# Two summing products turned round: one-pass transposes for the adaLN vectors, block-diagonal ones for the squares of queries and keys

## The chip, the core and the metric

The kernel runs on one NeuronCore of a Trainium2 chip. The metric is device time in microseconds (us), the median of the timed runs. The core's engines run side by side, each with its own instruction order fixed when the program is built: TensorE (PE in the profile, its weight loads PEld), VectorE (DVE), ScalarE (ACT), GpSimd (POOL) and SyncE (SP, which issues the transfers). They wait for each other through semaphores.

## The reference, cut to what matters

Two layers over 512 latent tokens with a prefix of 256 context tokens, width 1024: an attention layer, then a Mamba-2 layer, each followed by a gated feed-forward part. Before each part the activations are normalised and modulated by vectors that come from a conditioning vector:

```python
mod_l = jnp.split((silu_c @ ada_w[i] + ada_b[i])[:, None, :], 6, axis=-1)   # latent tokens
mod_c = jnp.split(silu_cc @ ada_w[i] + ada_b[i], 6, axis=-1)                # context tokens
h_l = modulate(rms_norm(x, norm_mix_w[i]), mod_l[0], mod_l[1])              # x * (1 + scale) + shift

# attention: each head of 64 of the queries (16 heads) and keys (4 heads) is normalised
q_l = rms_norm(q_l.reshape(bsz, seq, N_HEADS, HEAD_DIM), q_norm)
k_l = rms_norm(k_l.reshape(bsz, seq, N_KV_HEADS, HEAD_DIM), k_norm)
```

The change touches how the six modulation vectors of layer 0 are turned from a row into a column (five of them on TensorE), and how the squares of each head of 64 channels are summed for the norms of queries and keys.

## The kernel before, in words

Activations lie with channels on the 128 partitions and tokens along the free axis (512 latent, then 256 context). Large products run three times in a one-pass reduced type, on a high and a low part of each operand (`mm3`: lines L105, L106, L108); small ones run directly in float32, where the profile shows two weight loads and two products for each one in the program.

The first 72 us are the front of the attention layer, whose order on PE, ACT and DVE is written by hand (`manual_schedule`). A block of products `warm` runs while the first inputs arrive. Then, for each of the eight slabs m of 128 input channels: `ada` multiplies the conditioning vector (in `sc32`, columns 0 and 1 of 32: latent and context) with two blocks of 128 weight columns into the bank `ps_ada`, as four partial sums that lie on partitions 32j and 32j+1 for j = 0..3 (the k slabs of the contraction are dealt to four column strips of the array). DVE copies that to `ada_sb`. Then the four partial rows are added and turned into columns: one float32 product per 128 columns, with `ada_sb` as the stationary side and the 128x2 selector `g.sel` as the moving side, into `ps_adt` (L135). DVE adds the bias (`mod`, L146), forms the scale with the norm's weight (`moda`, L149) and modulates slab m of the activations: `ht` (L322, DVE), `hha` (L331, ACT), `hla` (L332, DVE). The six products `ps_l` of slab m consume `hha` and `hla`. The weights of each slab arrive as `wst` and are split into `wsh` (ACT) and `wsl` (POOL for seven slabs, DVE for the last). The same two steps run six more times in the attention stage for the other layer-0 vectors, as background jobs (`ps_ada` with 512 columns, four `ps_adt` products each).

From 72 us to about 330 us the order comes from a list scheduler with a cost model of its own: it places the context part `ps_c` of the projections, the values `ps_v`, the scores of each head pair (`ps_m` for their maxima, `ps_s`, exponentials `pr`), the product with the values (`ps_o`, L799: two products, one for each head of the pair, on the two halves of the array's columns), and in between the background jobs `ps_q`, `ps_ada`, `ps_adt` and the output projection `ps_d`. For each of ten pairs of heads (two of keys, eight of queries) `normed` squares the 128 channels on ACT and sums each head's 64 squares on TensorE into `ssq` (L677): a 64x64 block of ones for each head, 512 and then 256 columns, so four float32 products; the two heads' products lie on opposite quarters of the array. The later parts of the kernel are not touched.

Of the kernel before, what the change touches and what calls it, by code (L numbers as in the profile page):

```python
# [7 lines left out]
P = 128  # L8
F32 = mybir.dt.float32
# [3 lines left out]
AX = mybir.AxisListType  # L13
# [7 lines left out]
HD = 64  # L21
# [90 lines left out]
def ada(g, src, layer, chunks, m0, nm, big=True):  # L112


    nc = g.nc
    cols = nm * len(chunks) * P
    per = (1024 if big else T) // cols
    st = []
    for k0 in range(0, KT, per):
        n = min(per, KT - k0)  # L120
        t = t4(g, "wada") if big else t3(g, "wada")
        t = t[:, : n * cols].rearrange("p (k a b) -> p k a b", k=n, a=len(chunks))
        nc.sync.dma_start(t.rearrange("p k a b -> p (k a b)"), src[:, k0 * cols : (k0 + n) * cols])
        st += [t[:, k].rearrange("p a b -> p (a b)") for k in range(n)]
    yield 0
    ps = Bank(g, "ps_ada")
    for k in range(KT):
        j = k % 4
        nc.tensor.matmul(ps[32 * j : 32 * j + 32, 0:cols], g.sc32[:, k, :], st[k], start=k < 4, stop=k >= 4)
    sb = g.t3p.tile([P, 512], F32, tag="t2", bufs=6, name="ada_sb")  # L130
    nc.vector.tensor_copy(sb[:, 0:cols], ps[:, 0:cols])
    yield BREAK
    pt = Bank(g, "ps_adt")
    for i in range(cols // P):
        nc.tensor.matmul(pt[:, 2 * i : 2 * i + 2], sb[:, i * P : (i + 1) * P], g.sel, start=True, stop=True)  # L135
    for i, ch in enumerate(chunks):
        modulation(g, pt[:, 2 * nm * i : 2 * nm * (i + 1)].rearrange("p (m v) -> p m v", v=2), layer, ch, m0, nm)
    yield BREAK


def modulation(g, src, layer, ch, m0, nm, nv=2):

    nc = g.nc
    c0 = PC[f"adab{layer}"] + ch * KT + m0
    md = g.mod[layer][ch][:, m0 : m0 + nm, 0:nv]
    nc.vector.tensor_tensor(md, src, g.par[:, c0 : c0 + nm].unsqueeze(2).broadcast_to([P, nm, nv]), ALU.add)  # L146
    if ch in (1, 4):
        n0 = PC[("nmix" if ch == 1 else "nffn") + str(layer)] + m0
        nc.vector.scalar_tensor_tensor(g.moda[layer][ch][:, m0 : m0 + nm, 0:nv], md, 1.0,  # L149
                                       g.par[:, n0 : n0 + nm].unsqueeze(2).broadcast_to([P, nm, nv]),  # L150
                                       ALU.add, ALU.mult)
# [103 lines left out]
def ordered(g, bi, prev):  # L255

    if prev is not None:
        g.tc.add_manual_dep(bi.ins, prev.ins.name, mybir.DependencyInfo(
            mybir.DependencyClass.NoSync, mybir.DependencyReason.DATA), reason="place among products")
# [252 lines left out]
def attention(g, adas, project, X):  # L512


    nc, I = g.nc, g.I
# [45 lines left out]
    warm = Bk("warm")  # L561

    def busy(n):
        for _ in range(n):
            nc.tensor.matmul(warm[:, :P], g.ones, g.ones, start=True, stop=True)

    busy(38)
    acc = t3(g, "acc", n=L)
# [96 lines left out]
    def normed(qs, gain):  # L665

        sq = t3(g, "qsq")
        nc.scalar.activation(sq, qs, AF.Square)
        nc.scalar.activation(qs, qs, AF.Identity, scale=gain)
        sw = t2("qsw")  # L670
        for b in range(4):
            nc.sync.dma_start(sw[32 * (b ^ 1) : 32 * (b ^ 1) + 32], qs[32 * b : 32 * b + 32, :L])
        ss = []
        for c0, c1 in ((0, L), (L, T)):
            ps = Bk("ssq")
            for s in S64:
                ordered(g, nc.tensor.matmul(ps[s, : c1 - c0], g.ones[s, :HD], sq[s, c0:c1], start=True, stop=True), placed[0])  # L677
            ss.append((ps[:, : c1 - c0], slice(c0, c1)))
        nc.vector.tensor_tensor(qs[:, :L], qs[:, :L], g.cos, ALU.mult)
        nc.vector.tensor_tensor(sw, sw, g.sin, ALU.mult)  # L680
        nc.vector.tensor_tensor(qs[:, :L], qs[:, :L], sw, ALU.add)
        yield

        y, u = t3(g, "qy"), sq
        for ps, c in ss:
            nc.scalar.activation(y[:, c], ps, AF.Ln, scale=1.0 / HD, bias=eps64)
        nc.scalar.activation(y, y, AF.Exp, scale=-0.5)
        nc.scalar.activation(u, y, AF.Square)
        for ps, c in ss:
            nc.vector.scalar_tensor_tensor(u[:, c], ps, HD * EPS, u[:, c], ALU.add, ALU.mult)  # L690
        nc.vector.tensor_tensor(qs, qs, y, ALU.mult)
        nc.vector.scalar_tensor_tensor(qs, u, -3.0 * HD, qs, ALU.add, ALU.mult)
        yield
# [41 lines left out]
            nc.scalar.copy(qs[:, c0 : c0 + n], ps[:, :n])  # L735

    onesr = g.const.tile([P, P], F32R, name="onesr")
    nc.scalar.copy(onesr, g.ones)
    id2 = g.const.tile([P, HD], F32, name="id2")
    for h in S64:  # L740
        nc.gpsimd.tensor_copy(id2[h], g.ident[h, h])
# [796 lines left out]
def body(nc, tc, I, out, dbg=None):  # L1538
    g = Ctx()
# [16 lines left out]
    for m in range(0, KT, 2):  # L1556
# [1 line left out]
    nc.sync.dma_start(g.par, I["par"])  # L1558
    g.ident, g.blk, g.sel = (cst[:, a:b] for a, b in
                             ((CST_IDENT, CST_IDENT + P), (CST_BLK, CST_BLK + 2), (CST_SEL, CST_SEL + 2)))  # L1560
    g.ones = g.const.tile([P, P], F32, name="ones")
    nc.vector.memset(g.ones, 1.0)
    g.sc32 = g.const.tile([P, KT, 32], F32, name="sc32")
    nc.vector.memset(g.sc32, 0.0)
    tc.keep_in_program_order(nc.scalar.preload_act_table_set("natural_log_exp_and_others"))
# [154 lines left out]
```

## Time and profile before

| | |
|---|---|
| median of 3 runs | 1887.12 us (1885.73 to 1887.31) |
| span of the profiled execution, first to last instruction | 1884.5 us (its own time is not given apart from the span; the runs lie 1.2 to 2.8 us above it) |
| PE busy | 1860.0 us, 99% of the span, 10794 products |
| PEld / DVE / ACT / POOL busy | 81% / 72% / 44% / 12% |
| granted TensorE clock, mean | 1.000 |
| `ps_adt` on PE | 80 products, 16.4 to 283.0 us |
| `ssq` on PE | 80 products, 73.0 to 296.2 us |
| `warm` on PE | 98 products, 1.1 to 17.4 us |

A product's time in the table is from its start to its modelled end. Products overlap in the array, so what a product costs is the distance from its start to the next one's start, not its duration. In a timeline row the first number is the start in us, the second how long the merged group lasts, the numbers behind the operation its tile of the array (rows*columns) and the moving operand, and xN the number of merged instructions; the bracket gives the idle time of the engine before it and what ended that.

### The profile page before, as it was taken

The page shows a single profiled execution, that of the slowest core. Times are in us where ns is not written, and L with a number is a line of the kernel's source. Part 1 is how long each engine was busy: PE and PEld are TensorE (multiplying, and loading weights), DVE is VectorE, ACT ScalarE, POOL GpSimd, SP SyncE. Part 2 cuts the span into 40 slices and gives each one's busy share as a digit, 9 for nine tenths or more (in the row PEclk, how much of TensorE's full clock was granted, in tenths as well). Part 3 has the DMA queues.
Part 4 walks back from the last instruction along what each step waited for, and adds up shares of the span by engine and source line. Part 5 has one row for each costly group of instructions (what it writes and reads, how often), then busy time and mean ns, then how long its engine had stood idle before and what let it go on. Part 6 is the DMA issues. An engine that isn't in the chain of part 4 may idle for free.

```text
span 1884.5 us, 27447 instructions
## 1 busy us (share of the span) xinstructions
PE 1860.0 (99%) x10794; PEld 1531.3 (81%) x10794; DVE 1348.8 (72%) x2013; ACT 832.6 (44%) x1422; POOL 232.5 (12%) x220
## 2 busy tenths in 40 slices
PE   9999999999999999999999999999999999999999
PEld 7865545689888888888888888888887888888887
DVE  5688999678877777444478977777888676565655
ACT  3655544354222222222257577766667352323331
POOL 2100000030000000000031243443334200000000
PEclk9999999999999999999999999999999999999999
DMA  9223241015444554222224243434344323323332
GB/s 342 70 82 118 84 145 62 18 50 189 136 134 124 176 180 146 68 68 67 67 79 140 70 121 114 133 113 135 120 126 125 100 78 101 101 87 104 90 101 90
DMA packets 73489, 210.02 MB, mean 111 GB/s; under 512 B 8976, under 2 KB 14480, under 8 KB 73232
## 3 DMA queue, kind: packets, MB, share of 16 engines
q1 hardware_dynamic: 73360, 208.26, 35.2%
q8 instruction: 85, 1.39, 0.3%
q14 instruction: 44, 0.36, 0.1%
HBM read 198.79 MB, written 6.82 MB: 109 GB/s over the span
## 4 chain that ended last, share of the span: by engine, by line
PE 80%; DVE 10%; issue 4%; ACT 3%; DMA 2%; POOL 1%; SPq 0%; DVEq 0%; POOLq 0%; ACTq 0%
PE ps_up L105 10%; PE ps_up L106 10%; PE ps_up L108 10%; PE ps_d L105 6%; PE ps_d L108 6%; PE ps_d L106 5%; PE ps_in L105 4%; PE ps_in L108 4%; PE ps_in L106 3%; PE ps_o L799 2%; PE ps_s L835 2%; PE ps_st L1340 1%; DVE wl L87 1%; DVE xf L1212 1%; PE ps_wo L106 1%
## 5 line engine op out<-in xcount | busy, mean ns | idle before, releaser
L87 DVE TENSOR_TENSOR wl<-wst,wh 128x1024 fp32r<-128x1024 f32 x211 | 261.0, 1237 | 246.5 <-PE ps_up L106 125.4
L85 ACT CAST wh<-wst 128x1024 fp32r<-128x1024 f32 x211 | 220.8, 1048 | 413.5 <-DMA wst<-in_wup 316.2
L106 PE MATMUL ps_up<-hlf,wh 128*128 128x512 f32 x992 | 351.6, 354 | 0.0
L108 PE MATMUL ps_up<-hhf,wl 128*128 128x512 f32 x992 | 351.4, 354 | 0.0
L105 PE MATMUL ps_up<-hhf,wh 128*128 128x512 f32 x992 | 351.2, 355 | 0.0
L105 PEld LDWEIGHTS ps_up<-hhf,wh 128*128 128x128 f32 x992 | 187.5, 189 | 26.2
L106 PEld LDWEIGHTS ps_up<-hlf,wh 128*128 128x128 f32 x992 | 187.6, 189 | 26.0
L108 PEld LDWEIGHTS ps_up<-hhf,wl 128*128 128x128 f32 x992 | 187.5, 189 | 26.1
L105 PE MATMUL ps_in<-hhs,wh 128*128 128x512 f32 (+1 forms) x544 | 199.7, 367 | 0.0
L108 PE MATMUL ps_in<-hhs,wl 128*128 128x512 f32 (+1 forms) x544 | 193.5, 356 | 0.0
L106 PE MATMUL ps_in<-hls,wh 128*128 128x512 f32 (+1 forms) x544 | 193.3, 355 | 0.0
L108 PE MATMUL ps_d<-hdh,wl 128*128 128x512 f32 (+1 forms) x496 | 173.4, 350 | 0.0
L105 PE MATMUL ps_d<-hdh,wh 128*128 128x512 f32 (+1 forms) x496 | 173.3, 350 | 0.1
L106 PE MATMUL ps_d<-hdl,wh 128*128 128x512 f32 (+1 forms) x496 | 172.9, 349 | 0.0
L1022 DVE SCALAR_TENSOR_TENSOR X<-ps_d,mod,X 128x256 f32<-128x256 f32 (+1 forms) x176 | 102.7, 614 | 27.1 <-PE ps_d L108 27.0
L105 PEld LDWEIGHTS ps_in<-hhs,wh 128*128 128x128 f32 x544 | 102.8, 189 | 15.5 <-issue 1.9
L108 PEld LDWEIGHTS ps_in<-hhs,wl 128*128 128x128 f32 x544 | 102.7, 189 | 15.0
L106 PEld LDWEIGHTS ps_in<-hls,wh 128*128 128x128 f32 x544 | 102.9, 189 | 13.0
L106 PEld LDWEIGHTS ps_d<-hdl,wh 128*128 128x128 f32 x496 | 93.2, 188 | 14.4 <-DVE hdl L87 0.2
L108 PEld LDWEIGHTS ps_d<-hdh,wl 128*128 128x128 f32 x496 | 93.2, 188 | 13.1
L105 PEld LDWEIGHTS ps_d<-hdh,wh 128*128 128x128 f32 x496 | 93.0, 188 | 13.0 <-ACT hdh L85 0.3
L168 DVE SCALAR_TENSOR_TENSOR junk<-wada,cb 128x1024 f32<-128x1024 f32 x80 | 97.5, 1218 | 1.1 <-ACT cb L159 0.8
(375 smaller groups left out, 3632.9 us busy)
## 6 DMA issues: line engine op xcount, KB each, us to landing
wst<-in_wup SPq DMA_DIRECT2D x88, 512.0 KB, 3.5
wada<-in_adaT SPq DMA_DIRECT2D x56, 512.0 KB, 3.8
wst<-in_win SPq DMA_DIRECT2D x48, 512.0 KB, 3.6
wst<-in_wdown SPq DMA_DIRECT2D x44, 512.0 KB, 3.7
E<-ad SPq DMA_DIRECT2D x64, 256.0 KB, 6.7
wada<-in_adaB SPq DMA_DIRECT2D x24, 512.0 KB, 4.6
ec<-ead SPq DMA_DIRECT2D x64, 128.0 KB, 4.6
wst<-in_wout SPq DMA_DIRECT2D x16, 512.0 KB, 3.7
```

The source lines that it names most:

```text
L85: keep(nc.scalar.copy(hi, src))
L87: keep(eng.tensor_tensor(lo, src, _r(hi), ALU.subtract))
L105: mm(out, wh, ah, start=first, stop=False)
L106: mm(out, wh, al, start=False, stop=False)
L108: i = mm(out, wl, ah, start=False, stop=last)
L168: g.tc.keep_in_program_order(nc.vector.scalar_tensor_tensor(junk, w, 1.0, cb[:, v * D : (v + 1) * D], ALU.mult, ALU.mult, accum_out=md[:, ...
L799: nc.tensor.matmul(po[S64[e], :n], v, pr[:, 512 * e + off : 512 * e + off + n], start=first, stop=last)
L835: nc.tensor.matmul(outs[e], a[S64[e], k], b[S64[e], q], start=i == 0, stop=False)
L1022: nc.vector.scalar_tensor_tensor(ap, o[:, c0:c1], gate[:, m, v : v + 1], ap, ALU.mult, ALU.add)
L1212: i = nc.vector.scalar_tensor_tensor(cv, raw[:, tap : tap + n], par(f"sw{tap}", j), cv, ALU.mult, ALU.add)
L1340: nc.tensor.matmul(ps[:, d * 256 : (d + 1) * 256], Bt[:, t * P : (t + 1) * P], xw[d][t], start=t == ts[0], stop=t == ts[-1])
```

## The change

Modulation vectors: instead of the product with the selector, each 128 columns of `ada_sb` are transposed (`nc.tensor.transpose`, one instruction on PE where the product took two), and DVE adds the four partial sums of each vector straight out of PSUM with one `reduce_sum` per vector (22 in all) into `mod`. `modulation` then adds the bias with `mod` as input, in place, where its input was `ps_adt`.

Squares: a 128x128 matrix `heads` with two 64x64 blocks of ones on the diagonal replaces the two 64x64 products by one over the whole array. `heads` is made by three `memset`s on DVE. `ones` shrinks to 64 columns, `onesr` is therefore filled in two copies, and the products `warm` now use `heads` on both sides.

```diff
@@ ada
-        nc.tensor.matmul(pt[:, 2 * i : 2 * i + 2], sb[:, i * P : (i + 1) * P], g.sel, start=True, stop=True)
+        nc.tensor.transpose(pt[:, i * P : (i + 1) * P], sb[:, i * P : (i + 1) * P], g.ident)
+    quarters = pt[:, 0:cols].rearrange("p (m j r) -> p m r j", j=4, r=32)
     for i, ch in enumerate(chunks):
-        modulation(g, pt[:, 2 * nm * i : 2 * nm * (i + 1)].rearrange("p (m v) -> p m v", v=2), layer, ch, m0, nm)
+        md = g.mod[layer][ch][:, m0 : m0 + nm]
+        nc.vector.reduce_sum(md, quarters[:, nm * i : nm * (i + 1), 0:2], axis=AX.X)
+        modulation(g, md, layer, ch, m0, nm)
@@ attention, busy
-            nc.tensor.matmul(warm[:, :P], g.ones, g.ones, start=True, stop=True)
+            nc.tensor.matmul(warm[:, :P], g.heads, g.heads, start=True, stop=True)
@@ attention, normed
-            for s in S64:
-                ordered(g, nc.tensor.matmul(ps[s, : c1 - c0], g.ones[s, :HD], sq[s, c0:c1], start=True, stop=True), placed[0])
+            ordered(g, nc.tensor.matmul(ps[:, : c1 - c0], g.heads, sq[:, c0:c1], start=True, stop=True), placed[0])
@@ attention
-    nc.scalar.copy(onesr, g.ones)
+    for h in S64:
+        nc.scalar.copy(onesr[:, h], g.ones)
@@ body
-    g.ones = g.const.tile([P, P], F32, name="ones")
+    g.ones = g.const.tile([P, HD], F32, name="ones")
     nc.vector.memset(g.ones, 1.0)
+    g.heads = g.const.tile([P, P], F32, name="heads")
+    nc.vector.memset(g.heads, 0.0)
+    for h in (slice(0, HD), slice(HD, P)):
+        nc.vector.memset(g.heads[h, h], 1.0)
```

The scheduler also places some instructions elsewhere. Three places matter. The first is DVE in the hand-ordered front, slab 6, where `mod_86`/`mod_87` (after: `mod_90`/`mod_91`) are the shift and the scale. Before:

```order
L131 COPY ada_sb<-ps_ada 128x256
L146 TENSOR_TENSOR mod_86<-ps_adt,par 128x2
L146 TENSOR_TENSOR mod_87<-ps_adt,par 128x2
L149 SCALAR_TENSOR_TENSOR moda_98<-mod_87,par 128x2
L322 SCALAR_TENSOR_TENSOR ht<-X,moda_98,rsl 128x512
```

After:

```order
L131 COPY ada_sb<-ps_ada 128x256
L139 TENSOR_REDUCE mod_90<-ps_adt 128x2
L149 TENSOR_TENSOR mod_90<-mod_90,par 128x2
L139 TENSOR_REDUCE mod_91<-ps_adt 128x2
L149 TENSOR_TENSOR mod_91<-mod_91,par 128x2
L152 SCALAR_TENSOR_TENSOR moda_102<-mod_91,par 128x2
L325 SCALAR_TENSOR_TENSOR ht<-X,moda_102,rsl 128x512
```

Two instructions stand more between `ada_sb` and `ht`, and the two additions of the bias now read both inputs from SBUF (the row reads `mod,par` where it read `ps_adt,par`).

The second is PE in the attention stage near 256 to 262 us of the profile. `ps_o` is the product with the values, x2 the two heads of a pair. Before:

```order
L837 MATMUL ps_s<-diag_2389,onesr 128x512 x2
L799 MATMUL ps_o<-pr,v_752 64x512
L761 MATMUL ps_m<-kh_1991,qh 128x256 x4
L799 MATMUL ps_o<-pr,v_752 64x512
L835 MATMUL ps_s<-qh,kh_1991 128x512 x2
L835 MATMUL ps_s<-qh,kl_1992 128x512 x2
L835 MATMUL ps_s<-ql,kh_1991 128x512 x2
L837 MATMUL ps_s<-diag_2389,onesr 128x512 x2
L799 MATMUL ps_o<-pr,v_753 64x512
L761 MATMUL ps_m<-kh_1991,qh 128x512 x2
L799 MATMUL ps_o<-pr,v_753 64x512
```

After:

```order
L840 MATMUL ps_s<-diag_2397,onesr 128x512 x2
L764 MATMUL ps_m<-kh_2000,qh 128x256 x4
L802 MATMUL ps_o<-pr,v_772 64x512 x2
L838 MATMUL ps_s<-qh,kh_2000 128x512 x2
L838 MATMUL ps_s<-qh,kl_2001 128x512 x2
L838 MATMUL ps_s<-ql,kh_2000 128x512 x2
L840 MATMUL ps_s<-diag_2397,onesr 128x512 x2
L764 MATMUL ps_m<-kh_2000,qh 128x512 x2
L802 MATMUL ps_o<-pr,v_773 64x512 x2
```

Two pairs of `ps_o` that were parted by `ps_m` stand together now. The third is PE at the first background vector (near 163 us), where the opposite happens. Before:

```order
L837 MATMUL ps_s<-diag_1481,onesr 128x512 x2
L761 MATMUL ps_m<-kh_928,qh 128x512 x2
L135 MATMUL ps_adt<-cst,ada_sb 128x2 x4
L799 MATMUL ps_o<-pr,v_753 64x512 x2
L105 MATMUL ps_q<-hha_3_108,wh 128x512
```

After:

```order
L840 MATMUL ps_s<-diag_1492,onesr 128x512 x2
L802 MATMUL ps_o<-pr,v_773 64x512
L135 MATMUL ps_adt<-cst,ada_sb 128x128 x4
L764 MATMUL ps_m<-kh_945,qh 128x512 x2
L802 MATMUL ps_o<-pr,v_773 64x512
L105 MATMUL ps_q<-hha_3_112,wh 128x512
```

One pair of `ps_o` is parted by the four transposes and `ps_m`. At 62 to 64 us, where slab 7's `ps_l` products follow, 15 `ps_c` products stand ahead of the one that takes `hla` instead of 11. The order on SP and POOL is unchanged.

## The prediction

> **What bounds the kernel now.** I read the page first, then TensorE's waits by stage, then the timeline around the products that change.
>
> ```profile
> span 1884.5 us, 27447 instructions
> PE 1860.0 (99%) x10794; PEld 1531.3 (81%) x10794; DVE 1348.8 (72%) x2013; ACT 832.6 (44%) x1422; POOL 232.5 (12%) x220
> ```
>
> TensorE has work all the time, so a shorter product is worth its shortening wherever TensorE doesn't wait behind it. The waits in the two stages that change, 20 to 72 us and 72 to 330 us:
>
> ```profile
> PE ps_adt L135 <- DVE ada_sb L131: 1.3, 1, 1.3
> ...
> PE ps_l L106 <- DVE hla L332: 0.3, 1, 0.3
> ...
> PE ps_m L761 <- DVE ma L765: 3.3, 4, 1.2
> ```
>
> ```profile
> 110.00:330.00 220.00, 214.61 (x1336) 120.70 (x1334) 198.15 (x285) 115.19 (x154) 0.00 (x0) 1.00 0.31 102
> ```
>
> The first two rows are of the hand-ordered front and stand exactly on the chain that the change lengthens (modulation vector, then `ht`, `hha`, `hla`). The third is the largest wait of the attention stage, and the fourth row (columns: length, PE, PEld, DVE, ACT, POOL) says that TensorE is busy for 214.6 of 220 us there, DVE for 198.2. So the front is paced by DVE at two points, the attention stage by TensorE with a DVE close behind. Everything after 330 us only moves along.
>
> **Transposes in the attention stage** (six groups). Starts give the price:
>
> ```profile
> 187.19 1.08 PE L799 MATMUL ps_o<-pr,v 128*64 128x512 f32 x4
> 188.20 1.05 PE L135 MATMUL ps_adt<-cst,ada_sb 128*128 128x2 f32 x8
> 189.11 0.36 PE L105 MATMUL ps_q<-hha,wh 128*128 128x256 f32 x1
> 189.31 0.28 PE L106 MATMUL ps_q<-hla,wh 128*128 128x256 f32 x1
> 189.43 0.28 PE L108 MATMUL ps_q<-hha,wl 128*128 128x256 f32 x1
> ```
>
> ```profile
> 1017.32 1.47 PE L1314 MATMUL ps_xt<-cst,xf 128*128 128x128 f32 x12
> 1018.54 0.48 PE L105 MATMUL ps_in<-hhs,wh 128*128 128x512 f32 x1
> 1018.86 0.40 PE L106 MATMUL ps_in<-hls,wh 128*128 128x512 f32 x1
> 1019.09 0.40 PE L108 MATMUL ps_in<-hhs,wl 128*128 128x512 f32 x1
> ```
>
> From 188.20 to the second `ps_q` at 189.31 are 1.11 us; less 0.12 for one `ps_q` (189.31 to 189.43) the group costs 0.99 us for eight instructions (0.112 each, and 0.10 for the first weights after another tile of the array). Twelve float32 transposes of the same size, one instruction each, cost 1.54 us to the second `ps_in` less 0.23 for one `ps_in`: 1.31 us or 0.109 each. Four make 0.44 us against 0.90 for the eight: 0.46 us less a group, 2.8 us for six. Between the bounds nothing (rival C) and this I take this: the transposes of the row are of the same shape and type.
>
> **Transposes in the front** (eight groups of two): 4 x 0.112 less 2 x 0.109 is 0.23 us each, 1.8 us together, if TensorE set the pace there. It doesn't; see below.
>
> **Squares** (ten groups). Before, and the nearest float32 products over the whole array:
>
> ```profile
> 72.81 0.28 PE L108 MATMUL ps_c<-hha,wsl 128*128 128x256 f32 x1
> 73.02 1.51 PE L677 MATMUL ssq<-qsq,ones 64*64 64x512 f32 x8
> 74.46 0.39 PE L105 MATMUL ps_c<-hha,wsh 128*128 128x256 f32 x1
> 74.69 0.28 PE L106 MATMUL ps_c<-hla,wsh 128*128 128x256 f32 x1
> ...
> 295.03 1.51 PE L677 MATMUL ssq<-qsq,ones 64*64 64x512 f32 x8
> 296.46 0.50 PE L105 MATMUL ps_d<-hhol,wh 128*128 128x512 f32 x1
> 296.80 0.39 PE L106 MATMUL ps_d<-hlol,wh 128*128 128x512 f32 x1
> ```
>
> ```profile
> 1038.05 2.75 PE L1340 MATMUL ps_st<-xw,Bt 128*128 128x256 f32 x12
> 1040.45 0.47 PE L105 MATMUL ps_in<-hhs,wh 128*128 128x256 f32 x1
> 1040.76 0.28 PE L106 MATMUL ps_in<-hls,wh 128*128 128x256 f32 x1
> ```
>
> The two heads' products already run at the same time: the eight instructions (four of 512 columns, four of 256) take 1.44 us, and `ps_st` shows that one instruction of 256 float32 columns over the whole array takes (2.71 - 0.12) / 12 = 0.216 us. So the new group is not half as long: two of 512 columns at 0.43 and two of 256 at 0.216 make 1.29 us. What goes beside that is the change of tile: entering `ssq` from `ps_c` takes 0.21 us where 0.12 is usual, leaving it 0.23 where 0.12 is usual. In the three groups between `ps_c` or `ps_v` products the gain is 1.64 - 1.29 = 0.35 us. I count two of them, since the third ends in a wait for DVE (`qsq`) that takes the gain back. In four groups that come after another tile and are followed by full-array products, 1.43 + 0.11 (the 0.34 at 296.46 against 0.23) becomes 1.29 + 0.10 for the first weights: 0.15 less. In three groups between tiled products the 0.10 is new and the drain at the end stays: about 0.05 more. Sum 0.70 + 0.60 - 0.15 = 1.15 us. Its bounds are 10 x 0.35 and 10 x -0.05.
>
> **The moved products.** What a parted pair of `ps_o` costs:
>
> ```profile
> 256.45 1.07 PE L799 MATMUL ps_o<-pr,v 128*64 128x512 f32 x2
> 257.48 0.50 PE L761 MATMUL ps_m<-kh,qh 64*128 64x256 f32 x4
> 257.91 1.07 PE L799 MATMUL ps_o<-pr,v 128*64 128x512 f32 x2
> 258.91 0.50 PE L835 MATMUL ps_s<-qh,kh 64*128 64x512 f32 x2
> ```
>
> Each half alone takes 1.03 and 1.00 us; the whole pair at 187.19 took 1.01. A parted pair costs 1.0 us. Two are joined, one is parted: 1.0 us less, with bounds 0 (if TensorE waits there instead) and 2.0.
>
> **DVE's added work.** 22 sums and 22 additions where 22 additions stood. Six sums of the attention stage lie among 198 us of DVE work and nothing waits for these vectors; I cost them at nothing, and DVE's slack of 22 us is the cover. In the front they are on the chain:
>
> ```profile
> 53.01 0.23 DVE L146 TENSOR_TENSOR mod<-ps_adt,par 128x2 f32<-128x2 f32 x2 [1.46 <-PE ps_adt L135]
> 53.27 1.62 DVE L149 SCALAR_TENSOR_TENSOR moda<-mod,par 128x2 f32<-128x2 f32 x1
> ...
> 53.02 1.85 POOL L87 TENSOR_TENSOR wsl<-wst,wsh 128x768 fp32r<-128x768 f32 x1
> ...
> L149 DVE SCALAR_TENSOR_TENSOR moda<-mod,par x7: 160/161/1623, 21.8 to 61.3; 128x2 f32<-128x2 f32 x7
> ...
> 33.83 0.41 DVE L131 COPY ada_sb<-ps_ada 128x256 f32<-128x256 f32 x1
> ...
> 36.94 0.75 DVE L332 SCALAR_TENSOR_TENSOR hla<-ht,mod,hha 128x512 fp32r<-128x512 f32 x1 [0.79 <-ACT hha L331]
> ...
> 39.41 0.39 PE L106 MATMUL ps_l<-hla,wsh 128*128 128x512 f32 x1
> ```
>
> `mod` starts at 53.01, twice, and `moda` 0.26 us later; the new chain of sum, addition, sum, addition puts `moda` about 0.65 us behind the first sum (about 0.19 a dependent step: the 0.26 less some 0.07 by which the second `mod` starts behind the first), 0.38 more, less 0.12 since the transposes end sooner. [...] But `moda`, 128x2 elements with both inputs in SBUF, takes 1.62 us where 0.16 is usual (the row of all seven: least, middle and longest in ns) and ends at 54.89 when POOL's `wsl` ends at 54.87, while the two `mod`, which read PSUM, ran through. The new additions read both inputs from SBUF. So the first of them will stand where `moda` stood, and behind the end of `wsl` come an addition, a sum, an addition and `moda` instead of `moda` alone: 0.45 to 0.5 us a slab where POOL overlaps. [...]
>
> Where it reaches TensorE: slabs 1 and 2, with 0.45 each, push what ACT and DVE do behind them (the context's sums of squares) and so `ada_sb` at 33.83, for which `ps_adt` waits 1.3 us already, by about 0.8 less the little that other waits absorb; slabs 3 to 5 have slack (slab 3's `hla` ends at 37.69, its first product comes at 39.41) and give back 0.23 each; at slab 6 `hla` comes 0.9 to 1.0 later to a TensorE that already waits 0.3 for it; slab 7 adds 0.3 and gets 0.47 back, since four more `ps_c` of 0.12 now stand ahead of it. At 72 us I expect TensorE 0.8 us late, in place of the 1.8 early. Bounds: 1.8 early, and 1.8 late (half of one more `wsl` of 1.85 on the chain).
>
> **Start.**
>
> ```profile
> 1.05 11.33 PE L565 MATMUL warm<-ones 128*128 128x128 f32 x76 [1.05 <-DVE ones L1562]
> ...
> 1.05:4.05 3.00, 3.00 (x14) 3.00 (x15) 1.00 0.72 193
> 7.05:10.05 3.00, 3.00 (x29) 3.00 (x29) 1.00 1.06 335
> ```
>
> `heads` is ready about 0.45 us later than `ones` (three fills and `sc` ahead of it). The first products run at half speed (14 in 3 us against 29), so a late start costs 0.2 to 0.45 us; it is part of the 0.8.
>
> **Sum.** -2.8 - 1.15 - 1.0 + 0.8 = -4.1 us on the span, 1880.4. The median stands 2.6 us above the span, and I carry that over: 1887.1 - 4.1 = 1883.0 us. 0.2% (3.8 us) is about what a measurement of this kernel can tell from no change, so this is at the edge of being seen.
>
> **Rivals.**
> A. *DVE takes the gain back in the attention stage.* DVE is busy for 90% there, and `ps_m` waits for `ma` for 3.3 us already. If TensorE only arrives earlier at such waits, the transposes and the joined pairs (3.8 us) are lost: -1.15 + 0.8, 1886.7 us. Against it: the waits are 5.4 of 220 us.
> B. *The front hides the added steps* (the additions slip in ahead of `wsl`, as `mod` did at 53.01). Then its 1.8 us count as well: -2.8 - 1.15 - 1.0 - 1.8 = -6.8, 1880.4 us. Against it: POOL's `wsl` begins before or with the first `mod` in most slabs.
> C. *The transposes don't shorten anything*, because each takes its whole duration:
>
> ```profile
> L293 PE MATMUL rsTa<-cst,rba x6: 270/272/273, 16.0 to 43.9; 128*128 128x128 f32 x6
> ```
>
> At 0.272 us, four cost 1.09 us where eight products cost 0.99: +0.6 for six in place of -2.8, 1886.4 us. [...]
> D. *Slower: the clock is not granted in time.* `warm` now multiplies a half-empty matrix. If that didn't bring the full rate, the 76 products and the 22 after them would keep the 0.21 us of the first 3 us instead of 0.11: some 75 x 0.1 = 7.5 us more, and 1 to 1.5 for the first vectors; with the other terms 1887.1 - 4.1 + 8.5 = 1891.5 us. It decides from about 8 us of such delay on. Nothing in the rows says that the operands' values matter; the instructions are the same.
>
> **How the numbers follow.** Forecast as summed 0.55 (1881.2 to 1884.8, of which 0.36 lies beyond the 0.2% bound at 1883.35 and 0.19 within), A 0.20, B 0.14, C 0.03, D 0.04, and 0.04 for a moved instruction elsewhere that makes it slower. Faster 0.36 + 0.14 = 0.50; the same 0.19 + 0.20 + 0.03 = 0.42; slower 0.08. The range reaches to A at one end and B at the other: 1880.2 to 1887.0.
>
> **What would show it.** Right: `ps_adt` 40 products instead of 80, in groups of four taking 0.44 to 0.55 us; `ssq` 40, a group 1.29 us between `ps_c` products; one parted pair of `ps_o` instead of two; the wait of `ps_adt` for `ada_sb` near 34 us longer than 1.3, `hla` of slab 6 later than 57.2, additions of 128x2 with durations far over 0.16 that end with `wsl`; `ps_c`'s first `ssq` about 0.8 us later than 73.02. Wrong: that `ssq` earlier than 73.0 (B), waits for `ma`, `qsq` or PSUM in the attention stage of more than 9 us (A), `warm` products at 0.21 us beyond 7 us (D).

## The result, and the profile after

The changed kernel took 1892.82 us in the median of 14 runs (1888.06 to 1896.25), the kernel before 1887.47 in 14 runs on the same chip (1885.73 to 1890.02): a ratio of 1.0020 with a 95% interval of 1.0013 to 1.0028 (the two medians alone give the upper end). It is slower by 0.1 to 0.3%, where I forecast 1883.0 us. Its profiled execution took 1890.03 us, with a span of 1888.3 us, 3.8 us longer than before's. Of the runs in the experiments below four lasted 2267 to 6974 us; they are left out of the ratios and move the medians by less than 0.3 us. The first lines of the page show less work on TensorE and a longer span:

```profile
span 1888.3 us, 27311 instructions
PE 1856.5 (98%) x10714; PEld 1530.3 (81%) x10714; DVE 1353.2 (72%) x2038; ACT 832.3 (44%) x1423; POOL 233.0 (12%) x220
```

The products themselves cost what the prediction said. The timeline of TensorE at the first squares and at the background vector near 189 us:

```profile
73.65 1.45 PE L679 MATMUL ssq<-qsq,heads 128*128 128x512 f32 x4
74.76 0.47 PE L105 MATMUL ps_c<-hha,wsh 128*128 128x256 f32 x1
...
189.16 0.66 PE L135 MATMUL ps_adt<-cst,ada_sb 128*128 128x128 f32 x4
189.57 0.37 PE L105 MATMUL ps_q<-hha,wh 128*128 128x256 f32 x1
189.78 0.28 PE L106 MATMUL ps_q<-hla,wh 128*128 128x256 f32 x1
```

From 189.16 to the second `ps_q` at 189.78 are 0.62 us, less 0.11 for one `ps_q` (189.78 to the next at 189.89): 0.51 against 0.99 before. The squares take 1.11 us to the first `ps_c` plus its 0.31 less 0.12: 1.30 (1.29 was forecast). So TensorE gained 0.5 us a group of transposes and 0.3 us a group of squares between `ps_c` products, and the end is later all the same. The waits of TensorE (20 to 72 us, then 72 to 330 us; total, times, longest):

```profile
PE ps_adt L135 <- DVE ada_sb L131: 2.0, 1, 2.0
...
PE ps_m L764 <- DVE ma L768: 4.8, 4, 1.9
PE ps_d L105 <- DVE X L1025: 1.4, 1, 1.4
```

Here `ma` is DVE's maximum over `ps_m`, and `X` the activations to which DVE adds `ps_d`. All TensorE's waits from 72 to 330 us are 9.8 us, 5.8 before. And a column that stood at 1.00 everywhere in the trace of before now doesn't. The busy times by stretches (length, PE, PEld, DVE, ACT, POOL; the column behind POOL is the granted clock):

```profile
110.00:330.00 220.00, 210.92 (x1269) 119.06 (x1268) 196.02 (x290) 115.15 (x154) 0.00 (x0) 0.98 0.31 102
201.22:204.63 3.41, 1.75 (x7) 0.68 (x8) 2.81 (x4) 0.84 (x1) 0.00 (x0) 1.00 0.01 2
204.64:208.04 3.40, 3.40 (x14) 1.72 (x16) 1.13 (x2) 0.58 (x1) 0.00 (x0) 0.50 0.17 30
307.04:310.44 3.40, 1.97 (x14) 1.52 (x14) 3.31 (x10) 1.96 (x3) 0.00 (x0) 1.00 0.00 0
310.45:313.86 3.41, 3.41 (x17) 2.71 (x16) 3.13 (x6) 0.18 (x1) 0.00 (x0) 0.50 0.02 5
```

Twice TensorE runs at half clock for 3.41 us. Each time the 3.41 us ahead hold a long wait: TensorE is busy for 1.75 and 1.97 us of them. In the timeline one sees the wait, and then products of 0.43 us from start to start where 0.23 is usual:

```profile
202.88 0.50 PE L764 MATMUL ps_m<-kh,qh 64*128 64x512 f32 x2 [1.89 <-DVE ma L768]
...
204.65 0.63 PE L106 MATMUL ps_q<-hla,wh 128*128 128x512 f32 x1
205.08 0.63 PE L108 MATMUL ps_q<-hha,wl 128*128 128x512 f32 x1
```

Where the time goes is read from the start of the same product in two traces. The table gives the median difference to the kernel before, in us, over the 5 us from each mark on (the marks are times of before's trace); the columns behind the first are the experiments below ("q3" is the moved order near 163 us; the run with sums in PSUM is left out). "h" marks a row in which a half-clock stretch has been added since the row above.

| at | changed | mods alone | squares alone | q3 | fill | kl on POOL | reduced | reduced, kl on POOL | before, kl on POOL |
|---|---|---|---|---|---|---|---|---|---|
| 72 | +0.37 | +2.11 h | -0.01 | +1.70 h | +1.37 h | +0.47 | -0.35 | -0.49 | -0.32 |
| 113 | +0.22 | +2.53 | -0.19 | +1.84 | +1.58 | +0.30 | -0.44 | -0.52 | -0.02 |
| 150 | +0.46 | +2.53 | -0.14 | +2.24 | +1.97 | +0.73 | -0.41 | -0.47 | -0.02 |
| 165 | +1.14 | +2.10 | +0.93 | +1.96 | +2.67 | +1.42 | -0.74 | -0.77 | -0.05 |
| 190 | +0.48 | +1.61 | +0.78 | +1.31 | +2.31 | +1.28 | -1.23 | -1.25 | -0.03 |
| 200 | +1.14 | +2.28 | +0.86 | +2.06 | +3.06 | -0.21 | +0.06 h | -2.75 | -1.53 |
| 225 | +2.19 h | +1.79 | +0.87 | +1.58 | +2.56 | -0.70 | +0.35 | -3.26 | -1.54 |
| 270 | +0.62 | +0.16 | +0.93 | +2.28 h | +1.00 | -2.28 | -1.28 | -4.92 | -0.62 |
| 300 | +1.30 | +0.78 | +0.77 | +2.22 | +1.40 | -1.28 | -0.71 | -4.33 | -0.61 |
| 330 | +3.20 h | +0.79 | +0.78 | +4.24 h | +3.58 h | -0.85 | -0.76 | -4.39 | -0.60 |
| 1880 | +3.76 | +2.60 | +0.72 | +7.27 h | +5.39 | +1.03 | +1.22 | -2.77 | +1.33 |

Behind 330 us no changed instruction is left; a wait of `ps_xt` for `ec` at 1127 us, 0.7 us long in the trace of before, 1.3 after and up to 2.3 in others, makes most of the difference there in four of the traces (changed, mods alone, q3, reduced). In the changed kernel the two half-clock stretches are worth 1.6 and about 1.5 us of the 3.8. Beside them 0.7 us is lost at 163 us, 0.7 at 201 us, 0.7 between 270 and 300 us (where `ps_s` waits 0.8 us for DVE's `diag`, a wait that the trace of before doesn't have) and 0.4 in the longer wait for `X` near 310 us. What TensorE gained in between (0.65 from 165 to 190 us, 0.5 near 224 us, 1.6 from 255 to 270 us) doesn't make up for that.

Why TensorE waits 0.7 us longer at 201 us stands in DVE's timeline (`kl` is the low part of a pair of keys, `acc` the running sum of the exponentials `pr`), before:

```profile
195.44 3.85 DVE L706 TENSOR_TENSOR kl<-raw,kh 64x768 fp32r<-64x768 f32 x4
...
200.46 1.22 DVE L765 TENSOR_REDUCE ma<-ps_m 128x2 f32<-128x1024 f32 x1
```

and after:

```profile
196.58 3.84 DVE L708 TENSOR_TENSOR kl<-raw,kh 64x768 fp32r<-64x768 f32 x4
200.46 1.23 DVE L848 TENSOR_TENSOR acc<-acc,pr 128x1024 f32<-128x1024 f32 x1
201.60 1.22 DVE L768 TENSOR_REDUCE ma<-ps_m 128x2 f32<-128x1024 f32 x1
...
183.00:203.00 20.00, 18.11 (x109) 10.92 (x105) 18.64 (x24) 12.40 (x15) 0.00 (x0) 1.00 0.17 54
```

DVE goes from one instruction to the next here (18.64 of 20 us busy; it was as full before), 1.14 us later than before, and TensorE, only 0.5 late at 190 us, arrives early at a wait that ends when DVE does.

### The profile page after: what moved, and what is told of

Read it like the earlier page. It is cut to its first block, busy times and chain, and to the rows that moved or that the text cites. A ratio compares the mean times of both kernels' runs of the same rounds, so it can differ in the third digit from the quotient of the medians.

```text
span 1888.3 us, 27311 instructions
## 1 busy us (share of the span) xinstructions
PE 1856.5 (98%) x10714; PEld 1530.3 (81%) x10714; DVE 1353.2 (72%) x2038; ACT 832.3 (44%) x1423; POOL 233.0 (12%) x220
## 4 chain that ended last, share of the span: by engine, by line
PE 83%; DVE 9%; ACT 3%; DMA 2%; issue 2%; SPq 0%; POOL 0%; DVEq 0%; ACTq 0%; POOLq 0%
PE ps_up L105 10%; PE ps_up L106 10%; PE ps_up L108 10%; PE ps_d L105 5%; PE ps_d L108 5%; PE ps_d L106 5%; PE ps_in L105 5%; PE ps_in L108 5%; PE ps_in L106 5%; PE ps_st L1343 2%; PE ps_wo L106 1%; PE ps_wo L105 1%; PE ps_wo L108 1%; PE ps_o L802 1%; PE ps_yo L1408 1%
```

## The experiments

Theory 1: TensorE's gain turns into waits for a DVE that sets the pace for stretches of the attention stage, and a wait that is long enough brings 3.41 us at half clock behind it. Theory 2: DVE's added instructions cost a fixed amount, wherever they stand.

### Each half alone

The first kernel has the part of the diff in `ada` alone, the second the rest.

> Only the modulation vectors are turned by transposes and sums; squares and the products at the start as before. Theory 1 (TensorE's gain is lost in longer waits for DVE in the attention stage, and a wait of 1.4 us or more is followed by 3.41 us at half clock that cost 1.7 us more): ps_adt groups at 0.50 us in place of 0.99, waits of TensorE between 72 and 330 us of 6 to 10 us where before has 5.8, and a time of 1885 to 1891 us that follows from these waits and from the number of half-clock stretches. Theory 2 (the added sums and additions on DVE cost a fixed amount, the order of the products doesn't matter): the whole loss is here, 1892 to 1894 us.

Measured: 1888.66 us against 1888.14, ratio 1.0001 (0.9992 to 1.0010).

> Only the squares are summed by one product with block-diagonal ones (with the products at the start on heads); modulation vectors as before. Theory 1: the ssq groups gain their 1.2 us, DVE has no new work, but the order of the products in the attention stage moves again, so 1884.5 to 1889 us; half clock appears only behind a wait of 1.4 us or more. Theory 2: DVE has nothing new here, so the gain is all there is: 1886.0 to 1886.6 us and no half clock.

Measured: 1889.26 us, a little above what I expected, ratio 1.0005 (0.9995 to 1.0014). Theory 2 fails: neither half shows the loss, and the part without new work on DVE is no faster. In the table the squares alone gain 0.2 us up to 150 us and lose 1.07 between 150 and 165 us, where the order moved. The modulations alone have a wait of 2.6 us of `ps_adt` for `ada_sb` near 34 us, and half clock behind it. (This trace reached the full clock at 4.55 us, the changed kernel's at 6.66, where its `warm` products go from 0.21 to 0.11 us from start to start; so TensorE came to that wait earlier.) In the row 31.85 to 35.26 us TensorE is busy for 0.84 us:

```profile
31.85:35.26 3.41, 0.84 (x6) 0.40 (x4) 2.94 (x4) 0.11 (x1) 1.81 (x1) 1.00 1.03 403
35.27:38.67 3.40, 3.40 (x10) 2.75 (x9) 2.13 (x7) 0.72 (x1) 0.00 (x0) 0.50 1.02 395
```

Leaving those 1.7 us aside, the front costs some 0.8 us, and from 150 to 330 us 1.74 us are gained, most of it (1.63) where the two pairs of `ps_o` were joined.

### The additions of the bias from PSUM

```diff
-        md = g.mod[layer][ch][:, m0 : m0 + nm]
+        md = quarters[:, nm * i : nm * (i + 1), 4:6, 0]
         nc.vector.reduce_sum(md, quarters[:, nm * i : nm * (i + 1), 0:2], axis=AX.X)
```

> The whole change, but the sums are written to unused columns of ps_adt in PSUM, so that the additions of the bias read one operand from PSUM as before. If the additions stand still for POOL's wsl because both inputs are in SBUF, they take 0.25 us or less here and the first ssq comes 0.4 to 0.9 us earlier than at 73.65. Theory 1: what the front gains is not passed on as it is; the end moves with the waits for ma and the half-clock stretches, 1887 to 1893 us. Rival (the front's delay runs through to the end): 0.4 to 0.9 us below the changed kernel's 1892.8, with the same half-clock stretches.

Measured: 1898.07 us, above both forecasts, ratio 1.0049 (1.0036 to 1.0061). The groups of the front, least, middle and longest duration in ns, of the changed kernel and then of this one:

```profile
L149 DVE TENSOR_TENSOR mod<-mod,par x16: 160/161/1714, 17.4 to 62.4; 128x2 f32<-128x2 f32 x16
```

```profile
L149 DVE TENSOR_TENSOR mod<-ps_adt,par x16: 159/160/161, 17.9 to 62.8; 128x2 f32<-128x2 f32 x16
L152 DVE SCALAR_TENSOR_TENSOR moda<-mod,par x8: 161/162/1828, 18.5 to 63.0; 128x2 f32<-128x2 f32 x8
...
PE ssq L679 <- ACT qsq L671: 2.7, 1, 2.7
```

The additions stand still no longer, as expected, but `moda` now does (1828 ns). TensorE is no earlier at 72 us (+0.36 against +0.37). Whether the expected 0.4 to 0.9 us came is open all the same: this trace reached the full clock at 7.71 us, the changed kernel's at 6.66, and its TensorE is 0.49 us later from 8 to 18 us, so it regains about as much up to 72 us, and the trace doesn't tell whether by the edit or because the wait near 34 us swallowed the late start. What is lost behind it (+4.8 at 113 us) is the order again: several products were placed elsewhere from 64 us on, the third group of squares now waits 2.7 us for ACT near 113 us (a row of the waits, the last above), and half clock follows.

### What brings half clock

A program of its own: bursts of 32 one-pass products, and pauses that one DVE multiplication sets.

```diff
...
+            nc.vector.tensor_copy(big[:, 0:4], bank[:, 0:4])
+            nc.vector.tensor_tensor(r[:, : 64 + 160 * k], big[:, : 64 + 160 * k], big[:, : 64 + 160 * k], ALU.mult)
+            ...
+            nc.tensor.matmul(bank[:, :64], w, r[:, :64], start=True, stop=True)
+            for i in range(32):
+                nc.tensor.matmul(bank, w, x, start=True, stop=True)
```

> Not the computation: only bursts of 32 one-pass products of 512 columns (7 us) with 120 pauses of TensorE between them, set by one DVE multiplication of 64 to 1824 columns, so pauses of some 0.5 to 2.5 us, ten of each length; it writes ones. Theory 1: windows of 3.413 us at half clock, on a fixed grid, each behind a window of that grid in which TensorE stood still for some 1.4 us or more; pauses under 1.1 us never bring one, pauses over 2 us often do, depending on where they fall in the grid. Rival (only a pause of a whole window, 3.4 us, brings half clock, and the two stretches in the changed kernel have another cause): none behind any of these pauses.

Measured: 20 stretches of half clock, 19 of them 3.413 us long and one twice that, all on one grid of 3.413 us. A pair of windows of that grid (length, PE, PEld, DVE, POOL, clock), the pause in the first:

```profile
1021.83:1025.23 3.40, 1.39 (x7) 0.81 (x5) 1.94 (x2) 0.00 (x0) 1.00 0.00 0
1025.24:1028.65 3.41, 2.99 (x8) 2.44 (x9) 0.27 (x1) 0.00 (x0) 0.50 0.00 0
```

Read 0.2 us early, all 20 windows ahead of a stretch have 1.77 us or more of standing still and no other window has over 1.775. (The 0.2 us are fitted; read as they stand, the 20 still have 1.77 or more, but one window of 1.94 isn't followed by half clock.) So half of a window (1.77 of 3.413 us) is enough here, and it isn't the length of the pause alone: nine of the ten pauses of 1.94 us brought a stretch, none of the ten of 2.11 us, each of which the grid splits between two windows. No pause here is longer than 2.44 us, so the rival's pause of a whole window isn't needed.

> As the run with pauses alone, but between the pauses 56 products that fill the array less: in one half of the pauses two 64x128 tiles side by side (512 columns, as in ps_s), in the other half products of 256 columns over the whole array (as in ps_d). There the shortest pause in a window that brought half clock was 1.77 us, while in the kernels windows with 1.43 to 1.46 us did. If what counts is the work in the window and not the pause alone, half clock follows pauses of 1.4 to 1.7 us here in at least one of the two halves. Rival (only the pause counts): none below 1.75 us, as there.

The products between the pauses are those of the run above here, not the ones of the expectation, so this only repeats it: 24 stretches, four of them two windows long, again from 1.76 us on. The next run has the products that were meant:

```diff
...
+                if rep % 2:
+                    nc.tensor.matmul(bank[:, :256], w, x[:, :256], start=True, stop=True)
+                else:
+                    nc.tensor.matmul((other, bank)[i % 2], w[half[i % 2]], x[half[i % 2]], start=True, stop=True)
```

> Pauses of TensorE alone again, now with 56 products between them that use the array less: in one half of the pauses two 64x128 tiles side by side (512 columns, as in ps_s), in the other half products of 256 columns over the whole array (as in ps_d). With products of 512 columns over the whole array the shortest pause in a window that brought half clock was 1.77 us, in both runs; in the kernels a window with 1.46 us did and one with 1.82 us did not. If the work in the window counts and not the pause alone, the shortest pause with half clock is under 1.6 us in one of the two halves. Rival (only the pause counts): 1.7 to 1.8 us in both.

Measured: 49 stretches, two of them two windows long. With two 64-row tiles side by side 1.60 us of standing still brought half clock each time and 1.44 never; with 256 columns over the whole array 1.61 didn't, and 1.77 did in one window and not in three. The first pair of rows is of the tiles, the second of the whole array, with the same busy time:

```profile
63.51:66.92 3.41, 1.80 (x15) 1.25 (x15) 1.39 (x2) 0.00 (x0) 1.00 0.00 0
66.93:70.33 3.40, 3.40 (x20) 2.83 (x18) 0.00 (x0) 0.00 (x0) 0.50 0.00 0
172.73:176.15 3.42, 1.81 (x16) 1.64 (x15) 1.39 (x2) 0.00 (x0) 1.00 0.00 0
176.16:179.56 3.40, 3.40 (x30) 3.40 (x30) 0.00 (x0) 0.00 (x0) 1.00 0.02 5
```

The bound that I had set (under 1.6) was missed by 3 ns, and the rival's 1.7 by more: which products stand around the pause counts too. In the kernel three traces show half clock from 1.43 to 1.46 us at the wait of `ps_d` for `X`, but windows that, read in the same way, have 1.62 to 1.69 us of standing still near 1127 us (modulations alone, kl on POOL, reduced) and near 202 us (modulations alone) aren't followed by it. So no single bound holds in the kernel, and what else decides stays open.

### The wait filled with work

```diff
-                        for e in range(2):
-                            nc.tensor.matmul(outs[e], a[S64[e], k], b[S64[e], q], start=i == 0, stop=False)
+                        for r, e in enumerate([0, 1] * (1 + 3 * ((self.p, t, i) in FILL))):
+                            nc.tensor.matmul(outs[e], a[S64[e], k], b[S64[e], q], start=i == 0, stop=r < 6 * ((self.p, t, i) in FILL))
```

> The changed kernel with six products more: the first ps_s product of each head (pair 2, sixth step, ahead of the 1.89 us wait of ps_m for ma at 201 us) is issued four times instead of once, 0.7 us of work whose result is overwritten by the last one. All else keeps its order. Theory 1 (the wait is set by DVE; half clock comes behind a window of 3.41 us in which TensorE stood still too long): ps_m starts where it started, 202.9 within 0.15 us, the wait shrinks from 1.9 to 1.2 us, and no half-clock stretch follows there; more work, and yet 0.8 to 1.7 us less time than the changed kernel (about 1891.5). Rival (the stretch has another cause): it stays, and the time is 0 to 0.7 us above the changed kernel's 1892.8.

Measured: 1891.01 us against 1888.25, ratio 1.0011 (1.0002 to 1.0020; the changed kernel 1.0020, 1.0013 to 1.0028, so the two intervals overlap). The trace says more:

```profile
201.62 1.19 PE L838 MATMUL ps_s<-qh,kh 64*128 64x512 f32 x8
...
204.79 0.50 PE L764 MATMUL ps_m<-kh,qh 64*128 64x512 f32 x2 [1.28 <-DVE ma L768]
...
206.57 0.39 PE L106 MATMUL ps_q<-hla,wh 128*128 128x512 f32 x1
206.80 0.40 PE L108 MATMUL ps_q<-hha,wl 128*128 128x512 f32 x1
```

`ps_m` starts 1.91 us behind 202.88, and so does everything from 200 us on in this trace (+3.06 against +1.14, half clock near 35 us): the added products moved nothing. The wait is 1.28 us, and the clock stays whole (0.23 us from one `ps_q` to the next). From 200 to 210 us this kernel loses nothing (+3.06, +3.07), the changed one 1.6 (+1.14, +2.74).

### DVE relieved

```diff
-                nc.vector.tensor_tensor(l[to], qs[s], _r(h)[s], ALU.subtract)
+                (nc.gpsimd if j else nc.vector).tensor_tensor(l[to], qs[s], _r(h)[s], ALU.subtract)
```

> The changed kernel, but the four subtractions kl of the second pair of keys (4 x 0.95 us on DVE, 196.6 to 200.4) run on POOL, which has nothing to do there; the order of TensorE is the same to the last product. Theory 1 (DVE works without a gap from 184 to 203 us and sets the pace, so that TensorE's gain becomes a wait): the wait of ps_m for ma at 201 us falls from 1.89 to under 0.7 us, the half-clock stretch behind it is gone, TensorE is 2.5 to 3 us earlier at 215 us than in the changed kernel (1.2 from the wait, 1.7 from the clock), and the median falls by 1.5 to 3 us to about 1890.5. Rival (DVE has slack, the wait comes from the order of the products): the wait stays above 1.5 us and the time within 0.7 us of 1892.8. Against theory 1 would also be DVE's additions acc standing still while POOL works, up to 1.9 us each.

Measured: 1891.37 us, ratio 1.0010 (1.0001 to 1.0019). DVE and POOL at the place:

```profile
196.34 2.78 DVE L848 TENSOR_TENSOR acc<-acc,pr 128x1024 f32<-128x1024 f32 x1
199.04 1.21 DVE L768 TENSOR_REDUCE ma<-ps_m 128x2 f32<-128x1024 f32 x1
...
196.21 10.15 POOL L708 TENSOR_TENSOR kl<-raw,kh 64x768 fp32r<-64x768 f32 x4 [125.14 <-ACT kh L705]
...
201.62 0.40 PE L764 MATMUL ps_m<-kh,qh 64*128 64x512 f32 x2
```

The wait is gone, and with it the half clock: -0.21 at 200 us against +1.14, -0.15 against +2.74 at 210. `acc` stood still for 1.6 us while POOL worked, as feared, and it still paid. The profiled run has no half clock at all and a span of 1885.5 us; the median fell less than I expected. The waits for `X` (1.5 us) and `ada_sb` (2.0 us) are still there and may bring it in other runs (most of them have a clock of 0.997 to 0.999), which have no trace. The same edit in the kernel before:

> The kernel before with the four subtractions kl of the second pair of keys on POOL, nothing else; TensorE's order is that of the kernel before. Theory 1 (DVE sets the pace from 184 to 203 us in the kernel before already): the wait of 1.2 us for ma at 201 us goes, 1.0 to 1.5 us less at 215 us, 1886.5 to 1887.3 against the kernel before on the same chip. Rival (only the changed kernel is paced by DVE there): no difference beyond 0.3 us at 215 us.

Measured: 1.5 us less from 200 to 255 us, as theory 1 has it; 0.9 of it is lost again by 270 us (a wait of 0.84 us for `ma` that the kernel before doesn't have), and the time is the same (1887.80 against 1888.46, ratio 0.9998, 0.9988 to 1.0007). DVE sets the pace there in the kernel before too.

### The moved order near 163 us

```diff
-            ordered(g, nc.tensor.matmul(ps[:, : c1 - c0], g.heads, sq[:, c0:c1], start=True, stop=True), placed[0])
+            for s in S64 if qs is qraw.get(3) else (slice(0, P),):
+                ordered(g, nc.tensor.matmul(ps[s, : c1 - c0], g.ones[s] if qs is qraw.get(3) else g.heads, sq[s, c0:c1], start=True, stop=True), placed[0])
```

> The changed kernel, but one of the ten groups of squares (queries of pair 3) keeps the two 64x64 products. That alone gives the order near 163 us back: ps_m, then the four transposes, then the two ps_o together, and on DVE the addition acc behind qsq instead of ahead of it; the rest of TensorE's order is that of the changed kernel. Theory 1 (the moved order costs 1.0 to 1.1 us there and makes DVE late up to 203 us): TensorE at 165 to 180 us stands 0.0 to 0.3 us from the kernel before instead of 1.0 to 1.1, 0.8 to 1.2 less at 200 us too, for 0.15 us more in the squares; the waits for ma and X stay, so the half-clock stretches may too; 1891.5 on the median. Rival (the order doesn't matter, the squares' own length does): 0.15 us more than the changed kernel from 150 us on.

Measured: 1890.70 us, ratio 1.0006 (0.9996 to 1.0016). The place in this kernel, then in the changed one:

```profile
165.00 0.40 PE L765 MATMUL ps_m<-kh,qh 64*128 64x512 f32 x2
165.73 0.66 PE L135 MATMUL ps_adt<-cst,ada_sb 128*128 128x128 f32 x4 [0.33 <-DVE qsq L693]
166.31 1.08 PE L803 MATMUL ps_o<-pr,v 128*64 128x512 f32 x4
```

```profile
162.56 1.07 PE L802 MATMUL ps_o<-pr,v 128*64 128x512 f32 x2
164.48 0.66 PE L135 MATMUL ps_adt<-cst,ada_sb 128*128 128x128 f32 x4 [0.85 <-DVE qsq L692]
165.07 0.50 PE L764 MATMUL ps_m<-kh,qh 64*128 64x512 f32 x2
165.49 1.07 PE L802 MATMUL ps_o<-pr,v 128*64 128x512 f32 x2
```

Taking off its half clock near 36 us (1.7), it stands at +0.1 to +0.3 at 165 to 180 us where the changed kernel is at +1.0 to +1.1, and at +0.4 instead of +1.1 at 200 us. So the order costs 0.8 to 0.9 us here, not the products' length. The wait for `ma` at 201 us is no shorter for it (1.98 us in this trace), and the gain doesn't reach the end in this trace, which has four half-clock stretches. On DVE the moved order reads so, before and in the changed kernel: `acc` stands ahead of `mb` now and waits for `pr`.

```profile
159.73 1.22 DVE L765 TENSOR_REDUCE mb<-ps_m 128x4 f32<-128x1024 f32 x1
...
161.47 1.22 DVE L845 TENSOR_TENSOR acc<-acc,pr 128x1024 f32<-128x1024 f32 x1
```

```profile
160.87 1.22 DVE L848 TENSOR_TENSOR acc<-acc,pr 128x1024 f32<-128x1024 f32 x1 [0.59 <-ACT pr L841]
...
162.62 1.22 DVE L768 TENSOR_REDUCE mb<-ps_m 128x4 f32<-128x1024 f32 x1
```

### A reduced change, and one that is faster

Transposes for the six background vectors only, block-diagonal ones for the first three groups of squares only:

```diff
...
+        if big:
             nc.tensor.transpose(pt[:, i * P : (i + 1) * P], sb[:, i * P : (i + 1) * P], g.ident)
+        else:
+            nc.tensor.matmul(pt[:, 2 * i : 2 * i + 2], sb[:, i * P : (i + 1) * P], g.sel, start=True, stop=True)
...
```

> A reduced change: transposes and sums for the six background vectors of the attention stage alone (the eight slabs of the front keep the selector product, one DVE addition per vector), and block-diagonal ones for the three groups of squares between ps_c or ps_v products alone (the seven others keep two 64x64 products). Its order of TensorE is that of the kernel before, but for the two pairs of ps_o near 256 to 262 us that stand together. Theory 1: no late front, no parted ps_o at 163 us, so -0.2 us at 113 us (as with the squares alone) and -1.9 us at 330 us (as the part from 137 to 330 us with the modulations alone, -1.74): 2 us below the kernel before, 1885 to 1886.5 on the median if no wait exceeds 1.4 us. Rival (DVE takes back whatever TensorE gains in the attention stage): within 0.5 us of the kernel before.

Measured: 1887.50 us against 1888.25, ratio 0.9991 (0.9982 to 1.0000), above the 1885 to 1886.5 that I expected if no wait got too long. It is where theory 1 has it up to 190 us (-1.23). Then TensorE arrives at the wait for `ma`, which is 1.8 us long, and half clock follows:

```profile
201.07 0.80 PE L772 MATMUL ps_m<-kh,qh 64*128 64x512 f32 x2 [1.79 <-DVE ma L776]
...
197.62:201.03 3.41, 1.66 (x11) 0.79 (x9) 3.35 (x4) 2.07 (x3) 0.00 (x0) 1.00 0.00 0
201.04:204.45 3.41, 3.38 (x8) 1.24 (x9) 2.36 (x2) 0.00 (x0) 0.00 (x0) 0.50 0.00 0
```

> The reduced change of the run above, with the four subtractions kl of the second pair of keys on POOL. Theory 1: the wait for ma at 201 us (1.2 to 1.9 us) shortens to under 0.7, so 0.6 to 1.2 us less than the run above, 2.5 to 3.5 us below the kernel before. Rival (POOL's subtractions hold up DVE's additions of two operands in SBUF): no better than the run above.

Measured: 1883.04 us (1880.89 to 1884.39), ratio 0.9969 (0.9958 to 0.9981): faster than both kernels, 5.2 us below the one before, where I expected 2.5 to 3.5. TensorE has the same order as in the run above and no half-clock stretch. In the same windows:

```profile
199.09 0.40 PE L772 MATMUL ps_m<-kh,qh 64*128 64x512 f32 x2
...
197.62:201.03 3.41, 3.41 (x20) 1.66 (x19) 2.98 (x3) 1.92 (x3) 3.28 (x3) 1.00 0.00 0
```

The edit that was worth nothing to the end in the kernel before is worth 4.5 us here (1887.50 to 1883.04): about 1.8 us of wait, 1.7 of clock, and the rest later on (the wait for `ec` at 1127 us is 0.7 us here and 2.3 in the run above). All six runs read a mean granted clock of 1.000.

## Why the prediction was wrong, by its own steps

- **Transposes of the attention stage, -2.8.** The price was right: 0.5 us a group. The step that failed is that each shortening was booked to the end. At 190 us the gain is there (1.14 late at 165 us, 0.48 at 190), at 201 us DVE has taken it back (0.7 us), and so it does with the waits for `diag` at 277 us and `X` at 310 us (0.7 and 0.4 more). This is rival A, to which I gave 0.20.
- **"DVE's slack of 22 us is the cover."** That is the sum over 220 us. Where TensorE waits, DVE has next to none: 18.64 of 20 us busy from 183 us on. The sums themselves are small (0.15 to 0.18 us each); what made DVE late by 1.15 us is in the main the order at 163 us, where `acc` came to stand ahead of `mb`: with the old order back, 0.8 of TensorE's lateness at 200 us is gone. I had shown TensorE's rows of that place and not DVE's.
- **Squares, -1.15.** The groups cost 1.29 to 1.49 us as worked out, and the first three gave about what I counted (-0.2 to -0.4 us at 113 us beside a late start). But it was this part that moved the order near 163 us.
- **Moved products, -1.0.** The two joined pairs gave 1.6 us where I counted 2.0; the parted one cost 0.7 to 1.1 where I counted 1.0, the wait for `qsq` included.
- **Front, +0.8.** The first squares started at 73.65, 0.63 late. The additions stood still for POOL as the rows of `moda` had said (1714 ns at most, to 55.56 us, where `wsl` ends at 55.54). Whether that standing still is the cause of the lateness isn't shown: in the run with sums in PSUM it moved to `moda`, and that trace began 0.49 us later. So the size was about right, and its cause is open. The wait of `ps_adt` for `ada_sb` grew from 1.3 to 2.0 us as forecast, and I didn't see what that wait would trip.
- **The clock.** No term, and no rival outside the first microseconds: the second step that failed, and at 3.1 us of the 3.8 the larger one. In the trace of before no wait up to 330 us (1.3 us at most) brought half clock; of the four longest after (2.0, 1.89, 1.46 and 1.43) two did, the 1.89 and the 1.43. Each stretch costs 1.5 to 1.7 us, and the length of a wait alone doesn't say whether it brings one; in the program of pauses it depended on where the pause fell in the grid (nine of ten of 1.94 us did, none of ten of 2.11). In the changed kernel the two stretches begin 197.97 and 303.79 us behind the full clock, 58 and 89 times 3.413. The grid isn't tied to the kernel's start: the kernels' traces reached the full clock anywhere from 4.55 to 7.71 us, and of the six with the changed front the three that did so before 5.5 us (modulations alone, fill, q3) are the three with a stretch near 35 us. The kernel before isn't spared either: of its runs beside the first experiments 10 read a mean granted clock of 1.000 and nine 0.999 or 0.998, one 0.997 (1893.3 us); of the changed kernel's 14 runs none reads 1.000. These 14 spread over 8 us, and their median lies 2.8 us above the profiled run, which has two stretches. More stretches explain that in part only. The clock is 0.999 in the three shortest runs and 0.997 in the three longest, but the four runs about the median (1892.58 to 1892.95 us) read 0.998 and 0.999, one or two stretches. What else made those longer stays open, for they have no trace.

Rival A gave 1886.7 us. With two half-clock stretches that is 1890.1, near the profiled 1890.0, which is partly luck: A gives up the joined pairs too, while these gave 1.6 us and the waits for `diag` and `X` took 1.1. Its sign, more than 9 us of waits for `ma`, `qsq` or PSUM, was just missed: 8.7 us with the wait for `X`. D, the rival on the slower side, had the clock in it, but at the wrong place and for another reason: `warm` reached the full clock at 6.66 us (6.50 before).

## What to carry to other kernels

Slack that is averaged over a stage hides nothing at the wait that counts: read the busy time of the engine waited for in the 10 to 20 us ahead of each wait, and shorten that engine first, or together with the other. A wait of TensorE can have a second price: in these kernels some waits, the shortest of 1.43 us, were followed by 3.41 us at half clock, which cost 1.5 to 1.7 us, and it may be cheaper to fill such a wait with useless products than to leave it (from 200 to 210 us the filled kernel lost nothing, the changed one 1.6 us). Where a scheduler orders the work, compare the order of the engine that is waited for, not only that of the bound.

## What the runs showed of the hardware that I had not expected

- Half clock came after as little as 1.43 us of standing still in a window of 3.413 us and lasted one window, rarely two (7 of the 93 stretches in the three programs of pauses). From what length on it came differs with the products around the pause (1.60 us with pairs of 64-row tiles, 1.77 with the whole array), and in the kernel no single length decides (1.43 us brought it, windows with 1.62 to 1.69 didn't).
- Four subtractions of 64x768 elements took 10.15 us on POOL where DVE took 3.84; and a DVE addition of 1.22 us with both operands in SBUF took 2.78 beside them (two more 1.47 each), while a reduction from PSUM kept its 1.21.
